# Attention over ragged batches: the transpose of x moves from TensorE to the DMA crossbar, behind a casting load

## Chip, cores, metric

The kernel runs on one core of one Trainium2 chip. The metric is the device time of one execution in microseconds (us). Every comparison is with runs of the kernel before on the same chip. The engines are called by the names of the profile: PE (TensorE), PEld (its weight loads), DVE (VectorE), ACT (ScalarE), POOL (GpSimd), SP (the queue that issues DMAs here).

## The reference

There are 32 batches of 512 rows and 512 columns, with 8 heads of 64. Rows past a batch's length count neither as keys nor in the output. Input and output are float32.

```python
for b in range(batch):
    x_b = x[b, :lengths[b]]
    q, k, v = np.split(np.matmul(x_b, w_qkv), 3, axis=-1)      # then split into heads
    scores = scale * np.matmul(q, k.transpose(0, 2, 1))
    attn = softmax(scores)
    output[b, :lengths[b]] = np.matmul(attn, v)                # heads side by side
```

## The kernel before

The program is a software pipeline over batches: step i projects batch i, attends over batch i-1 and normalizes and stores batch i-2. The Tile framework orders the instructions of each engine by itself, so the order on an engine is not the order of the text.

```python
    # ... pools: ps_a 4 PSUM buffers (psa), ps_s 2 (pssc); bx, bqk, bav, bo, epool in SBUF ...
    def dma_x(j, first=False):
        if j < B:
            xnat[j] = bx.tile([P, NT, D], FP32, tag="x_nat", bufs=4, name="x_nat")
            nc.sync.dma_start(out=xnat[j], in_=x[j].rearrange("(t p) d -> p t d", p=P))

    def stage_qkv(b):
        dma_x(b + 3)
        x_nat = xnat[b]
        x16 = bx.tile([P, NT, D], F16, tag="x16")
        nc.vector.tensor_copy(out=x16, in_=x_nat)                     # DVE cast
        xT = bx.tile([P, NC, MAXS], F16, tag="xT")
        for c in range(NC):
            pxt = ps_a.tile([P, NT, P], F16, tag="psa")
            for t in range(NT):
                nc.tensor.transpose(pxt[:, t, :], x16[:, t, c * P : (c + 1) * P], ident_f16)
            nc.scalar.copy(out=xT[:, c, :], in_=pxt.rearrange("p t q -> p (t q)"))
        for m in range(2 * NC):
            pq = ps_a.tile([P, MAXS], FP32, tag="psa")                # 4 matmuls over c
            # ...
            nc.vector.tensor_copy(out=qkT[:, m, :], in_=pq)
        # ... v: 4 tiles pv of 4 matmuls each, masked by DVE into v_aug ...

    def stage_attn(b):
        def emit_scores(i):                # a pair of heads
            ep = epool.tile([P, 2, NT, MAXS], F16, tag="et")
            for kt in range(NT):
                psc = ps_s.tile([P, 2, MAXS], FP32, tag="pssc")
                # ... two matmuls psc, one for each head ...
                nc.scalar.activation(out=ep[:, :, kt, :], in_=psc, func=AF.Exp, scale=scale)
        # ... emit_av(i): 8 matmuls pav, DVE copies them into avout ...

    def stage_out(b):
        # ... 32 PE transposes pot, DVE: den, rcp, out_nat (product) ...
        nc.sync.dma_start(out=out[b].rearrange("(t p) d -> p t d", p=P), in_=out_nat)
```

The names in what follows: pxt are the transposes of x and xT their copies; pq and pv are the projections; psc are the scores, ep their exps; pav is the weighted sum over v and avout its copy; pot are the transposes of the output and out_nat the normalized output. A transition is the stretch from the last pav of one attention to the pq of the next batch.

The softmax here doesn't subtract the row's maximum and nothing guards it: scores larger than these inputs give would overflow.

Of the kernel before, what the change touches and what calls it, by code (L numbers as in the profile page):

```python
# [9 lines left out]
FP32 = mybir.dt.float32  # L10
F16 = mybir.dt.float16
# [4 lines left out]
P = 128  # L16
# [5 lines left out]
def kernel(  # L22
# [8 lines left out]
    nc = tc.nc  # L31
    B, MAXS, D = x.shape
    NT = MAXS // P
    NC = D // P
# [5 lines left out]
    bx = ctx.enter_context(tc.tile_pool(name="bx", bufs=2))  # L40
# [5 lines left out]
    ps_a = ctx.enter_context(tc.tile_pool(name="ps_a", bufs=4, space=bass.MemoryType.PSUM))  # L46
    ps_s = ctx.enter_context(tc.tile_pool(name="ps_s", bufs=2, space=bass.MemoryType.PSUM))

    xnat = [None] * B

    def dma_x(j, first=False):
        if j < B:
            xnat[j] = bx.tile([P, NT, D], FP32, tag="x_nat", bufs=4, name="x_nat")
            nc.sync.dma_start(
                out=xnat[j], in_=x[j].rearrange("(t p) d -> p t d", p=P)
            )

    dma_x(0)
    len64 = const.tile([1, B], mybir.dt.int64)
    nc.sync.dma_start(out=len64, in_=lengths.unsqueeze(0))  # L60
    dma_x(1)
    dma_x(2)

    ident = const.tile([P, P], FP32)
    make_identity(nc, ident)
    ident_f16 = const.tile([P, P], F16)
# [4 lines left out]
    for c in range(NC):  # L71
# [18 lines left out]
        out=kmask,  # L90
# [6 lines left out]
        out=qbig,  # L97
# [8 lines left out]
    avout_t = [None] * B  # L106

    def stage_qkv(b):
        dma_x(b + 3)
        x_nat = xnat[b]  # L110
        x16 = bx.tile([P, NT, D], F16, tag="x16")
        nc.vector.tensor_copy(out=x16, in_=x_nat)  # L112

        xT = bx.tile([P, NC, MAXS], F16, tag="xT")
        for c in range(NC):
            pxt = ps_a.tile([P, NT, P], F16, tag="psa")
            for t in range(NT):
                nc.tensor.transpose(  # L118
                    pxt[:, t, :], x16[:, t, c * P : (c + 1) * P], ident_f16
                )  # L120
            nc.scalar.copy(out=xT[:, c, :], in_=pxt.rearrange("p t q -> p (t q)"))  # L121

        qkT = bqk.tile([P, 2 * NC, MAXS], F16, tag="qkT")
        qkT_t[b] = qkT
        for m in range(2 * NC):
            pq = ps_a.tile([P, MAXS], FP32, tag="psa")
            for c in range(NC):
                nc.tensor.matmul(  # L128
                    pq,
                    w_r[:, c, m * P : (m + 1) * P],  # L130
                    xT[:, c, :],
                    start=(c == 0),
                    stop=(c == NC - 1),
                )
            nc.vector.tensor_copy(out=qkT[:, m, :], in_=pq)  # L135

        v_aug = bav.tile([P, NT, NH, HD + 1], F16, tag="vaug")
        vaug_t[b] = v_aug
        for t in range(NT):
            pv = ps_a.tile([P, D], FP32, tag="psa")  # L140
            for c in range(NC):
                nc.tensor.matmul(  # L142
                    pv,
                    xT[:, c, t * P : (t + 1) * P],
                    w_r[:, c, 2 * D : 3 * D],
                    start=(c == 0),
                    stop=(c == NC - 1),
                )
            nc.vector.tensor_scalar_mul(  # L149
                v_aug[:, t, :, 0:HD],  # L150
                pv.rearrange("p (h d) -> p h d", d=HD),
                kmask[:, t, b : b + 1],
            )
        nc.vector.tensor_copy(  # L154
            out=v_aug[:, :, :, HD],
            in_=kmask[:, :, b].unsqueeze(2).broadcast_to([P, NT, NH]),
        )
# [52 lines left out]
    def stage_out(b):  # L210
        avout = avout_t[b]
        avout_t[b] = None
        out_nat = bo.tile([P, NT, D], FP32, tag="out_nat")
        for qt in range(NT):
            den8 = sml.tile([P, NH], FP32, tag="den8")
            rcp8 = sml.tile([P, NH], FP32, tag="rcp8")
            pot = ps_a.tile([P, NH, HD + 2], F16, tag="psa")
            for h in range(NH):
                nc.tensor.transpose(  # L219
                    pot[:, h, 0 : HD + 1],  # L220
                    avout[0 : HD + 1, h, qt * P : (qt + 1) * P],
                    ident_f16[0 : HD + 1, 0 : HD + 1],
                )
            nc.vector.tensor_scalar(
                out=den8,
                in0=pot[:, :, HD],
                scalar1=qbig[:, qt, b : b + 1],
                scalar2=None,
                op0=ALU.add,
            )  # L230
            nc.vector.reciprocal(out=rcp8, in_=den8)
            nc.vector.tensor_tensor(  # L232
                out=out_nat[:, qt, :].rearrange("p (h d) -> p h d", d=HD),
                in0=pot[:, :, 0:HD],
                in1=rcp8.unsqueeze(2).broadcast_to([P, NH, HD]),
                op=ALU.mult,
            )
        nc.sync.dma_start(out=out[b].rearrange("(t p) d -> p t d", p=P), in_=out_nat)

    for i in range(B + 2):  # L240
        if i < B:
            stage_qkv(i)
        if 1 <= i <= B:
            stage_attn(i - 1)
        if i >= 2:
            stage_out(i - 2)
# [3 lines left out]
_INS = ['x', 'w_qkv', 'lengths', 'n_heads']  # L250
_OUTS = [((32, 512, 512), 'float32')]
#: Inputs that are plain numbers.
_NUMBERS = {'n_heads': 8}


# [26 lines left out]
```

## Time and profile before

The first three runs gave a median of 948.09 us (946.94 to 950.38). The profiled one has a span of 945.1 us.

| what | before | read from |
|---|---|---|
| PE, ACT, DVE busy | 94%, 58%, 63% | page, busy time |
| two periods of the pipeline (two batches) | 56.43 us | timeline: starts of pv |
| pq and pv of a batch on PE | 6.6 us, 3.45 us | chain of waits |
| one exp in an unbroken row | 0.925 us (12.02 us for 13) | timeline of ACT |
| first pv starts at | 32.18 us | timeline |

The page, cut: the engines' busy time; the one DMA queue of the loads and stores (packets, MB, share of the DMA engines' time); the chain that ended last, by engine and by line.

```profile
PE 891.2 (94%) x5120; PEld 363.4 (38%) x5120; DVE 592.6 (63%) x1094; ACT 547.5 (58%) x645; POOL 1.1 (0%) x8
...
q1 hardware_dynamic: 34370, 70.26, 21.2%
...
PE 83%; ACT 10%; DVE 3%; issue 2%; DMA 1%; POOLq 0%; ACTq 0%; POOL 0%
PE pav L190 25%; PE pq L128 23%; PE psc L173 18%; PE pv L142 12%; ACT ep L180 8%; PE pxt L118 3%; DVE avout L197 2%; PE pot L219 2%; ACT xT L121 2%; DMA w_f<-in_w_qkv_dram 1%; DVE out_nat L232 0%; ACT w_r L74 0%; POOLq L277 0%; ACTq L180 0%; DVE iota_f L86 0%
```

PE is busy nearly throughout, so what it is busy with is what counts; but the profile models the ends of matmuls, and a busy PE that moves at the pace of another engine looks the same. So read the time order as well. The batches come in two kinds of transition, because the order on PE alternates. PE, timeline before, first kind (start, duration, engine, line, operation, output and inputs, shape, count; in brackets idle time and who ended it):

```profile
402.13 0.61 PE L173 MATMUL psc<-qkT 64*128 64x512 f16 x4
402.90 0.40 PE L118 MATMUL pxt<-ident_f_95,x_3802 128*128 128x128 f16 x4 [0.17 <-DVE out_nat L232]
...
403.83 0.39 PE L173 MATMUL psc<-qkT 64*128 64x512 f16 x2
404.17 0.87 PE L118 MATMUL pxt<-ident_f_95,x_3802 128*128 128x128 f16 x8
...
405.59 0.37 PE L173 MATMUL psc<-qkT 64*128 64x512 f16 x1
405.90 6.65 PE L128 MATMUL pq<-xT,w_r 128*128 128x512 f16 x30
```

And the second kind, from the first pxt on:

```profile
431.97 0.40 PE L118 MATMUL pxt<-ident_f_95,x_4081 128*128 128x128 f16 x4
...
432.62 0.40 PE L118 MATMUL pxt<-ident_f_95,x_4081 128*128 128x128 f16 x4
...
433.27 0.80 PE L118 MATMUL pxt<-ident_f_95,x_4081 128*128 128x128 f16 x8
433.91 1.03 PE L128 MATMUL pq<-xT,w_r 128*128 128x512 f16 x4
```

In both, the 16 transposes pxt are mixed with the first score matmuls psc of the next attention, and the projection pq comes behind. ACT over the same stretch:

```profile
402.62 1.02 ACT L180 ACTIVATE ep<-psc 128x1024 f16<-128x1024 f32 x1 [2.68 <-PE psc L173]
403.54 1.07 ACT L121 COPY xT<-pxt 128x512 f16<-128x512 f16 x2
404.49 1.05 ACT L180 ACTIVATE ep<-psc 128x1024 f16<-128x1024 f32 x1
405.40 1.11 ACT L121 COPY xT<-pxt 128x512 f16<-128x512 f16 x2
...
416.36 12.02 ACT L180 ACTIVATE ep<-psc 128x1024 f16<-128x1024 f32 x13 [8.92 <-PE psc L173]
...
445.27 11.11 ACT L180 ACTIVATE ep<-psc 128x1024 f16<-128x1024 f32 x12 [8.81 <-PE psc L173]
```

ACT's four xT copies stand among the exps of the transition.

### The profile page before, as it was taken

How to read it: one execution, taken by the hardware profiler on the slowest of the kernel's cores; microseconds unless marked ns; L12 is line 12 of the kernel's file. 1: busy time of each engine (PE TensorE's matmuls, PEld its weight loads, DVE VectorE, ACT ScalarE, POOL GpSimd, SP SyncE). 2: the span in 40 equal slices, each digit the busy share in tenths (PEclk: the TensorE clock that was granted, in tenths of full speed). 3: DMA queues.
4: the chain of work that ended last, by engine and by line, in shares of the span. 5: the costliest groups of instructions: out<-in, count | busy, mean ns of one | idle time of the engine just before them, and what ended most of it. 6: DMA issues, size and time to landing. Idle time of an engine off the chain costs nothing.

```text
span 945.1 us, 12346 instructions
## 1 busy us (share of the span) xinstructions
PE 891.2 (94%) x5120; PEld 363.4 (38%) x5120; DVE 592.6 (63%) x1094; ACT 547.5 (58%) x645; POOL 1.1 (0%) x8
## 2 busy tenths in 40 slices
PE   2999999999999999999999999999999999999995
PEld 1433434433334433334433334433334433344332
DVE  2745667756667665567756667665566656666555
ACT  3177555576565567455576565567554575645764
POOL 0000000000000000000000000000000000000000
PEclk9899999999999999999999999999999999999997
DMA  9410222220222220222220222220122110111102
GB/s 330 159 45 1 89 89 89 90 72 31 76 90 89 89 89 23 68 90 89 90 72 32 76 89 90 89 82 25 72 90 89 45 45 1 45 45 45 45 26 108
DMA packets 34426, 71.05 MB, mean 75 GB/s; under 512 B 1090, under 2 KB 1090, under 8 KB 34370
## 3 DMA queue, kind: packets, MB, share of 16 engines
q1 hardware_dynamic: 34370, 70.26, 21.2%
q8 instruction: 40, 0.66, 0.3%
q14 instruction: 16, 0.13, 0.0%
HBM read 36.70 MB, written 33.55 MB: 74 GB/s over the span
## 4 chain that ended last, share of the span: by engine, by line
PE 83%; ACT 10%; DVE 3%; issue 2%; DMA 1%; POOLq 0%; ACTq 0%; POOL 0%
PE pav L190 25%; PE pq L128 23%; PE psc L173 18%; PE pv L142 12%; ACT ep L180 8%; PE pxt L118 3%; DVE avout L197 2%; PE pot L219 2%; ACT xT L121 2%; DMA w_f<-in_w_qkv_dram 1%; DVE out_nat L232 0%; ACT w_r L74 0%; POOLq L277 0%; ACTq L180 0%; DVE iota_f L86 0%
## 5 line engine op out<-in xcount | busy, mean ns | idle before, releaser
L180 ACT ACTIVATE ep<-psc 128x1024 f16<-128x1024 f32 x512 | 484.1, 1072 | 355.1 <-PE psc L173 355.1
L197 DVE CAST avout<-pav 65x512 f16<-65x512 f32 x256 | 172.9, 686 | 243.5 <-PE pav L190 243.5
L190 PE MATMUL pav<-ep,v_aug 128*65 128x512 f16 x1024 | 297.0, 388 | 0.0
L128 PE MATMUL pq<-xT,w_r 128*128 128x512 f16 x1024 | 239.5, 388 | 7.3 <-ACT w_r L74 7.2
L173 PE MATMUL psc<-qkT 64*128 64x512 f16 x1024 | 215.5, 385 | 17.0 <-ACT ep L180 13.1
L135 DVE CAST qkT<-pq 128x512 f16<-128x512 f32 x256 | 171.2, 689 | 58.9 <-PE pq L128 57.2
L128 PEld LDWEIGHTS <-w_r 128*128 128x128 f16 x1024 | 98.3, 100 | 128.6 <-issue 16.6
L190 PEld LDWEIGHTS <-v_aug 128*65 128x65 f16 x1024 | 84.2, 110 | 125.7 <-issue 100.1
L173 PEld LDWEIGHTS <-qkT 64*128 64x128 f16 x1024 | 60.5, 93 | 180.3 <-issue 170.9
L142 PE MATMUL pv<-w_r,xT 128*128 128x512 f16 x512 | 115.7, 379 | 0.0
L149 DVE TENSOR_SCALAR v_aug<-pv,kmask 128x512 f16<-128x512 f32 x128 | 96.4, 753 | 16.0 <-PE pv L142 5.5
L121 ACT COPY xT<-pxt 128x512 f16<-128x512 f16 x128 | 70.6, 603 | 22.6 <-PE pxt L118 22.0
L142 PEld LDWEIGHTS <-xT 128*128 128x128 f16 x512 | 50.1, 98 | 60.4
L219 PE MATMUL pot<-ident_f_95,avout 65*128 65x65 f16 x1024 | 45.9, 194 | 2.8 <-DVE out_nat L232 1.4
L219 PEld LDWEIGHTS <-avout 65*128 65x128 f16 x1024 | 38.9, 98 | 19.6 <-issue 7.8
L118 PE MATMUL pxt<-ident_f_95,x_129 128*128 128x128 f16 x16 | 1.9, 308 | 11.7 <-DVE ident_f_95 L67 11.7
L74 ACT CAST w_r<-w_f 128x1536 f16<-128x1536 f32 x4 | 5.8, 1488 | 5.3 <-DMA w_f<-in_w_qkv_dram 5.3
L154 DVE CAST v_aug<-kmask 128x32 f16<-128x32 f32 x32 | 7.4, 230 | 0.0
L118 PEld LDWEIGHTS <-x_129 128*128 128x128 f16 x16 | 1.7, 142 | 11.6 <-DVE x_129 L112 7.4
L112 DVE CAST x_129<-x_nat 128x2048 f16<-128x2048 f32 x1 | 1.2, 1227 | 6.1 <-DMA x_nat<-in_x_dram 6.1
L89 DVE TENSOR_TENSOR kmask<-iota_f,len_f 128x128 f32<-128x128 f32 x1 | 0.3, 292 | 5.1 <-POOL len_f L81 5.1
L86 DVE CAST iota_f<-iota_i 128x4 f32<-128x4 int32 x1 | 0.2, 246 | 3.8 <-POOL iota_i L84 3.8
(490 smaller groups left out, 262.4 us busy)
## 6 DMA issues: line engine op xcount, KB each, us to landing
x_nat<-in_x_dram SPq DMA_DIRECT2D x32, 1024.0 KB, 6.5
out_dram<-out_nat SPq DMA_DIRECT2D x32, 1024.0 KB, 4.9
w_f<-in_w_qkv_dram SPq DMA_DIRECT2D x4, 768.0 KB, 8.9
len_84<-in_lengths_dram SPq DMA_DIRECT2D x1, 0.2 KB
```

What stands on the lines that cost most here:

```text
L118: nc.tensor.transpose(pxt[:, t, :], x16[:, t, c * P : (c + 1) * P], ident_f16)
L121: nc.scalar.copy(out=xT[:, c, :], in_=pxt.rearrange("p t q -> p (t q)"))
L128: nc.tensor.matmul(pq, w_r[:, c, m * P : (m + 1) * P], xT[:, c, :], start=(c == 0), stop=(c == NC - 1),)
L135: nc.vector.tensor_copy(out=qkT[:, m, :], in_=pq)
L142: nc.tensor.matmul(pv, xT[:, c, t * P : (t + 1) * P], w_r[:, c, 2 * D : 3 * D], start=(c == 0), stop=(c == NC - 1),)
L149: nc.vector.tensor_scalar_mul(v_aug[:, t, :, 0:HD], pv.rearrange("p (h d) -> p h d", d=HD), kmask[:, t, b : b + 1],)
L154: nc.vector.tensor_copy(out=v_aug[:, :, :, HD], in_=kmask[:, :, b].unsqueeze(2).broadcast_to([P, NT, NH]),)
L173: nc.tensor.matmul(psc[:, par, :], qkT[rq : rq + 64, NC + i, kt * P : (kt + 1) * P], qkT[rq : rq + 64, i, :], start=True, stop=True,)
L180: nc.scalar.activation(out=ep[:, :, kt, :], in_=psc, func=AF.Exp, scale=scale)
L190: nc.tensor.matmul(pav[0 : HD + 1, :], v_aug[:, kt, h, :], ep[:, par, kt, :], start=(kt == 0), stop=(kt == NT - 1),)
L197: nc.vector.tensor_copy(out=avout[0 : HD + 1, h, :], in_=pav[0 : HD + 1, :])
L219: nc.tensor.transpose(pot[:, h, 0 : HD + 1], avout[0 : HD + 1, h, qt * P : (qt + 1) * P], ident_f16[0 : HD + 1, 0 : HD + 1],)
```

## The change

Its intent is to take 16 transposes a batch off PE, four PSUM copies off ACT and one cast off DVE, and to let the DMA engines do all three. The load is issued on POOL's queue and casts to fp16; four crossbar transposes on SP's queue then build xT. The Trainium skill, "DMA: Bandwidth & Descriptors", section "SWDGE vs HWDGE vs iDMA", ties the cast to POOL's queue and the plain transpose to SP's or ACT's, which is why two queues are needed. Stores move to POOL's queue as well, so that they don't stand between transposes.

```diff
     def dma_x(j, first=False):
         if j < B:
-            xnat[j] = bx.tile([P, NT, D], FP32, tag="x_nat", bufs=4, name="x_nat")
-            nc.sync.dma_start(
-                out=xnat[j], in_=x[j].rearrange("(t p) d -> p t d", p=P)
-            )
+            x16 = bx.tile([P, NT, D], F16, tag="x16", bufs=3, name="x16")
+            nc.gpsimd.dma_start(
+                out=x16, in_=x[j].rearrange("(t p) d -> p t d", p=P)
+            )
+            xT = bx.tile([P, NC, MAXS], F16, tag="xT", bufs=3, name="xT")
+            for t in range(NT):
+                nc.sync.dma_start_transpose(
+                    out=xT[:, :, t * P : (t + 1) * P], in_=x16[:, t, :]
+                )
+            xnat[j] = xT
 # ... dma_x(2) at the start goes away ...
     def stage_qkv(b):
-        dma_x(b + 3)
-        x_nat = xnat[b]
-        # ... cast, 16 transposes, 4 copies, as above ...
+        dma_x(b + 2)
+        xT = xnat[b]
 # ...
-        nc.sync.dma_start(out=out[b].rearrange("(t p) d -> p t d", p=P), in_=out_nat)
+        nc.gpsimd.dma_start(out=out[b].rearrange("(t p) d -> p t d", p=P), in_=out_nat)
```

More of the change, by code (lines that the diff above doesn't have):

```diff
@@ L61 @@
     dma_x(1)
-    dma_x(2)
     ident = const.tile([P, P], FP32)
@@ L108, in stage_qkv @@
     def stage_qkv(b):
-        dma_x(b + 3)
-        x_nat = xnat[b]
-        x16 = bx.tile([P, NT, D], F16, tag="x16")
-        nc.vector.tensor_copy(out=x16, in_=x_nat)
-        xT = bx.tile([P, NC, MAXS], F16, tag="xT")
-        for c in range(NC):
-            pxt = ps_a.tile([P, NT, P], F16, tag="psa")
-            for t in range(NT):
-                nc.tensor.transpose(
-                    pxt[:, t, :], x16[:, t, c * P : (c + 1) * P], ident_f16
-                )
-            nc.scalar.copy(out=xT[:, c, :], in_=pxt.rearrange("p t q -> p (t q)"))
+        dma_x(b + 2)
+        xT = xnat[b]
         qkT = bqk.tile([P, 2 * NC, MAXS], F16, tag="qkT")
```

## The prediction

> **What bounds the kernel now.** The page gives PE 94% busy, ACT 58%, DVE 63%, DMA about a fifth; granted clock 0.98. The timeline shows a period of 56.4 us for two batches (28.2 us each). One batch on PE: query/key projection (pq) 6.6 us and value projection (pv) 3.45 us, both back to back on PE; attention, 12.5 to 13 us, in which a pair of psc and two pav take 0.92 us, which is also ACT's pace for one exp (12.0 us for 13), so PE and ACT are about even there; and a transition of about 5 us: 32 pot transposes, 16 pxt transposes, the next batch's first psc pairs. In the transition the chain of waits goes PE psc, ACT ep, ACT xT, ACT ep, PE pq: the xT copies stand between the exps that free psc's two buffers. Over the span the chain has pxt with 3% and xT with 2%.
>
> **What the change removes.** Per batch: 16 pxt on PE (four take 0.33 to 0.38 us on the chain, so about 1.4 us), 4 xT copies on ACT (pairs of 0.97 to 1.1 us, so about 2.1 us), one DVE cast of 1.23 us (DVE has idle time: worth nothing). PE's order in the built program shows the rest unchanged: pot, three psc, pq, pv.
>
> Critical share: even batches go from psc at 402.2 through two exps and two copies to pq at 405.9; without the copies and pxt only one exp (1.02 us) is left before the third psc, so about 1.8 us is saved. Odd batches: pq starts at 434.07, and would start at about 432.4: 1.6 us. Estimate 1.7 us x 32 = 54 us.
>
> **What it adds.** Per batch one casting load on GpSimd's queue (1 MB read, 0.5 MB written) and four crossbar transposes of 128x512 fp16 on SP's. No trace here has a crossbar transpose. The Trainium skill, "VectorE: DVE Perf Modes", section "The three transpose paths", gives 1309 ns for 128x128 by DMA crossbar and 390 ns on TensorE. Estimate from it: at worst 16 x 1.31 = 21 us a batch if nothing overlaps, under the 26.5 us period left. With three xT buffers, the transposes of batch j start when pq/pv of batch j-3 is done, about two periods ahead. So I expect them hidden and PE never waiting for xT in the steady state. The output leaves through GpSimd behind loads that were ready earlier; no stall expected.
>
> Start: PE's first full pq group waits for the last w_r cast (25.4 us). In the new order on SP the last two w_f loads stand behind eight transposes, which wait for two GpSimd loads. Before, they were issued at 15.8 us; I expect 16 to 22. Cost 0 to 8 us, say 3. End: the last output through GpSimd, about 1 us more.
>
> **Prediction.** 948 - 54 + 3 + 1 = 898 us, 80% range 884 to 917. Faster by over 2%: 0.87; within 2%: 0.06; slower: 0.07.
>
> **What would show it right.** Timeline: period near 26.5 us; pxt and xT gone; ACT's exps in the transition back to back; PE's waits name no DMA apart from the start. DMA view: four transposes of a batch landing within about 20 us. Start: last w_r cast between 25 and 33 us.
>
> **What would make it wrong.** Transposes of over 6.6 us each, in series: then PE waits for xT in every batch and the kernel is DMA-bound, perhaps slower than before. SP's issue of the transposes taking microseconds each, delaying the weights. Slow casting loads. Or the transition being held by the DVE chain (den, rcp, out_nat, 3.4 us), which frees the PSUM buffers that pq takes: then the gain is nearer 1 us a batch.

## More of the kernel before

A period is the time from the first pv of a batch to the first pv of the next; it is called undisturbed where no stretch of half clock falls into it.

After pv, exps run in one unbroken row: 13 of them in 12.02 us after the first kind of transition, 12 in 11.11 us after the second.

## The result, and the profile after

The changed kernel took 904.66 us (median of 4 runs, 900.37 to 906.16), the kernel before in the same rounds 948.51 us. The ratio is 0.9529, with a 95% interval of 0.9499 to 0.9558. The profiled span fell from 945.1 to 903.6 us.

The page after, the same parts (POOL's queue is q0, SP's is q1):

```profile
PE 852.7 (94%) x4608; PEld 332.8 (37%) x4608; DVE 551.1 (61%) x1062; ACT 484.4 (54%) x517; POOL 49.5 (5%) x72
...
q0 software_dynamic: 25600, 50.34, 22.5%
q1 hardware_dynamic: 70210, 19.94, 11.2%
...
PE 53%; issue 21%; ACT 18%; DVE 3%; DMA 2%; SPq 1%; POOL 1%; POOLq 0%; ACTq 0%
```

PE is as busy as before, in share. The DMA engines went from 21.2% to 33.7% (both queues), and PE waits for them only at the start. That is read from PE's own waits (who waited for whom: us in total, times, longest us):

```profile
PE pq L122 <- DMA xT<-x_82: 16.4, 1, 16.4
PE psc L167 <- ACT ep L174: 9.3, 17, 0.9
PE pq L122 <- ACT w_r L79: 7.1, 2, 6.9
```

The only wait for a DMA, 16.4 us, is the start; so is the third line, where the casts of w_r wait for the last loads of the weights. How fast the crossbar works is seen in two timelines. SP's queue, the four transposes of a batch, and POOL's queue, the load that waits until they have freed x16:

```profile
399.55 5.12 SPq L59 DMA_TRANSPOSE xT<-x_3757  x4
```

```profile
406.45 0.74 POOL L54 DMA_DIRECT2D x_4528<-in_x_dram  x1 [15.87 <-DMA xT<-x_3757]
```

SP issues four transposes in 5.12 us, and the load that waits for their completion is released at 406.45, 6.9 us after the first was issued. A period is 27 us, so the crossbar needs a quarter of it.

PE after, the end of the two kinds of transition:

```profile
415.02 0.60 PE L167 MATMUL psc<-qkT 64*128 64x512 f16 x3
415.71 1.89 PE L122 MATMUL pq<-xT,w_r 128*128 128x512 f16 x8
...
441.44 0.39 PE L167 MATMUL psc<-qkT 64*128 64x512 f16 x2
442.32 0.37 PE L167 MATMUL psc<-qkT 64*128 64x512 f16 x1 [0.50 <-ACT ep L174]
442.63 7.08 PE L122 MATMUL pq<-xT,w_r 128*128 128x512 f16 x32
```

ACT after:

```profile
427.01 12.02 ACT L174 ACTIVATE ep<-psc 128x1024 f16<-128x1024 f32 x13 [9.63 <-PE psc L167]
441.25 1.94 ACT L174 ACTIVATE ep<-psc 128x1024 f16<-128x1024 f32 x2 [2.21 <-PE psc L167]
453.52 12.94 ACT L174 ACTIVATE ep<-psc 128x1024 f16<-128x1024 f32 x14 [10.33 <-PE psc L167]
```

pxt and the copies are gone, and pq follows psc at once (in the first kind one last psc, at 417.53, stands between the pq groups). But compare the unbroken rows of exps. After the first kind of transition there are 13 again (12.02 us), after the second kind there are now 14 (12.94 us) where there were 12. What this does is seen in the chain of waits over that one period, with the row of 12 before (441.2 to 468.8) and the row of 14 after (449.5 to 476.7):

```profile
by line: PE pav L190 25.2%; PE pq L128 24.6%; PE psc L173 16.5%; PE pv L142 12.5%; ACT ep L180 10.8%; DVE avout L197 4.9%; ACT xT L121 3.5%; PE pot L219 1.5%; issue 1.1%; ACTq L180 0.1%
by line: ACT ep L174 45.2%; PE pq L122 27.2%; PE pv L136 12.7%; DVE avout L191 4.7%; issue 3.0%; DVE out_nat L226 2.5%; PE psc L167 2.4%; PE pav L184 1.4%; DVE den_4214 L218 0.5%; DVE den_4228 L218 0.5%; DVE rcp_4215 L225 0.4%
```

Before, attention on the chain is PE's psc and pav; after, in this period, it is ACT's exps. In the period with the row of 13 the chain goes over psc and pav after the change too (ACT ep 7.8%).

The starts of pv, read from the timeline, give the account of the profiled runs:

| stretch | before | after | difference | predicted |
|---|---|---|---|---|
| to the first pv | 32.18 | 34.92 | +2.7 | +3 |
| first to last pv (31 periods) | 866.44 | 820.69 | -45.8 | -54 (32 x 1.7) |
| last pv to the end | 46.48 | 47.99 | +1.5 | +1 |

The undisturbed periods alternate. Before they are 28.86 and 27.57 us, after 26.51 and 27.14 us; the mean falls from 28.22 to 26.83, by 1.39 us. Some periods are longer by 1.3 to 1.7 us. They are told under the first experiment.

### The profile page after: what moved, and what is told of

Its sections match the earlier page's. It is cut to its first block, busy times and chain, and to the rows that moved or that the text cites. A ratio compares the mean times of both kernels' runs of the same rounds, so it can differ in the third digit from the quotient of the medians.

```text
span 903.6 us, 11385 instructions
## 1 busy us (share of the span) xinstructions
PE 852.7 (94%) x4608; PEld 332.8 (37%) x4608; DVE 551.1 (61%) x1062; ACT 484.4 (54%) x517; POOL 49.5 (5%) x72
## 4 chain that ended last, share of the span: by engine, by line
PE 53%; issue 21%; ACT 18%; DVE 3%; DMA 2%; SPq 1%; POOL 1%; POOLq 0%; ACTq 0%
PE pq L122 21%; ACT ep L174 18%; PE pav L184 13%; PE pv L136 10%; PE psc L167 9%; DVE avout L191 2%; PE pot L213 1%; SPq L59 1%; DVE out_nat L226 1%; DMA x_82<-in_x_dram 1%; DMA w_f<-in_w_qkv_dram 1%; POOL out_dram L232 1%; ACT w_r L79 0%; POOLq L271 0%; DVE qkT L129 0%
## 5 line engine op out<-in xcount | busy, mean ns | idle before, releaser
L174 ACT ACTIVATE ep<-psc 128x1024 f16<-128x1024 f32 x512 | 477.2, 1082 | 382.8 <-PE psc L167 382.8
L191 DVE CAST avout<-pav 65x512 f16<-65x512 f32 x256 | 169.7, 684 | 271.6 <-PE pav L184 271.5
L184 PE MATMUL pav<-ep,v_aug 128*65 128x512 f16 x1024 | 305.0, 389 | 1.5
L122 PE MATMUL pq<-xT,w_r 128*128 128x512 f16 x1024 | 238.8, 390 | 24.8 <-DMA xT<-x_82 16.4
L184 PEld LDWEIGHTS <-v_aug 128*65 128x65 f16 x1024 | 80.5, 110 | 124.4 <-issue 109.7
L213 PE MATMUL pot<-ident_f_103,avout 65*128 65x65 f16 x1024 | 50.7, 194 | 2.3 <-DVE out_nat L226 1.6
L213 PEld LDWEIGHTS <-avout 65*128 65x128 f16 x1024 | 41.6, 98 | 27.6 <-issue 14.6
L232 POOL DMA_DIRECT2D out_dram<-out_nat x32 | 24.3, 761 | 431.7 <-DVE out_nat L226 410.0
L54 POOL DMA_DIRECT2D x_1444<-in_x_dram x1 | 0.7, 740 | 25.4 <-DMA xT<-x_673 25.4
L54 POOL DMA_DIRECT2D x_7098<-in_x_dram x1 | 0.7, 740 | 17.2 <-DMA xT<-x_6327 17.2
L54 POOL DMA_DIRECT2D x_4528<-in_x_dram x1 | 0.7, 740 | 15.9 <-DMA xT<-x_3757 15.9
```

What stands on the lines that cost most here:

```text
L122: nc.tensor.matmul(pq, w_r[:, c, m * P : (m + 1) * P], xT[:, c, :], start=(c == 0), stop=(c == NC - 1),)
L184: nc.tensor.matmul(pav[0 : HD + 1, :], v_aug[:, kt, h, :], ep[:, par, kt, :], start=(kt == 0), stop=(kt == NT - 1),)
L191: nc.vector.tensor_copy(out=avout[0 : HD + 1, h, :], in_=pav[0 : HD + 1, :])
L213: nc.tensor.transpose(pot[:, h, 0 : HD + 1], avout[0 : HD + 1, h, qt * P : (qt + 1) * P], ident_f16[0 : HD + 1, 0 : HD + 1],)
L232: nc.gpsimd.dma_start(out=out[b].rearrange("(t p) d -> p t d", p=P), in_=out_nat)
```

## The experiments

Three questions: which of the things removed was worth the 1.39 us; which half of the change did it; and what holds the period now. The theory at the start (A) was that of the prediction: copies and transposes shared the critical path in the transition. The rivals: PE alone (B), since 16 pxt, at 0.33 to 0.38 us for four on the chain, are about 1.4 us by themselves; and the queues and the DVE cast (C).

All runs, ratios to the kernel before. "Period" is the mean of the undisturbed periods; "half clock" counts the stretches of half clock on PE between 40 us and the last attention, in the profiled execution alone.

| run | median us | ratio, 95% interval | period us | half clock | first pv us |
|---|---|---|---|---|---|
| before | 947.4 to 948.7 | 1 | 28.22 | 5 | 32.2 |
| the change | 904.7 | 0.953 (0.950 to 0.956) | 26.83 | 3 | 34.9 |
| e1_pe_back | 946.0 | 0.999 (0.997 to 1.000) | 27.83 | 9 | 34.2 |
| e2_act_back | 904.9 | 0.955 (0.953 to 0.958) | 26.82 | 1 | 36.7 |
| e3_cast_only | 942.7 | 0.995 (0.992 to 0.998) | 28.22 | 6 | 26.0 |
| e4_xbar_only | 909.2 | 0.960 (0.958 to 0.962) | 27.05, see there | 3 | 33.1 |
| e5_w_on_act | 897.2 | 0.946 (0.942 to 0.949) | 26.82 | 1 | 30.0 |
| e6_half_exp (wrong result) | 853.0 | 0.898 (0.894 to 0.902) | 25.32 | 0 | 37.7 |
| e7_spread | 878.3 | 0.926 (0.922 to 0.929) | 26.10 | 0 | 34.9 |
| e8_spread_w | 873.6 | 0.921 (0.917 to 0.924) | 26.10 | 0 | 30.7 |
| e9_before_spread | 927.4 | 0.977 (0.974 to 0.981) | 27.81 | 0 | 33.2 |
| e10_both_free | 957.2 | 1.008 (1.003 to 1.013) | 28.06 | 11 | 35.0 |

### e1_pe_back: PE's transposes put back, nobody reads them

```diff
         xT = xnat[b]
+        for c in range(NC):
+            pxt = ps_a.tile([P, NT, P], F16, tag="psa")
+            for t in range(NT):
+                nc.tensor.transpose(pxt[:, t, :], x16s[b][:, t, c * P : (c + 1) * P], ident_f16)
```

> The changed kernel with the 16 TensorE transposes of each batch put back; what they write is read by nobody, so ACT's copies stay away. Result correct. Theory A (the gain comes from the transition between two batches, where PE's transposes and ACT's copies shared the critical path): part of the 44 us comes back, 10 to 30 us, so 914 to 934 us. Rival B (PE alone: 16 transposes at 0.087 us are 1.4 us, which is all that a batch became shorter): all comes back, 940 to 950 us. Rival C (the gain comes from the loads and stores leaving SP's queue and from the DVE cast): nothing comes back, 900 to 909 us.

Measured: 945.98 us, as rival B has it. But the period tells more than the time: it is 27.83 us, so the undisturbed period went up by 1.0 us, not by 1.39. That is a mean over two orders on PE. All periods of this run have the order of the second kind (13 exps in the row, PE waits 0.50 us for an exp in the transition); beside the changed kernel's period of that kind, 26.51 us, the 16 pxt cost 1.32 us, all of it between the last pav and the next pv, so nearly their whole time on PE. The rest of the 41 us comes from nine stretches in which PE had half its clock, against three in the changed kernel's profile. One of them, by windows of one us (from:to, length, busy time of each engine, granted clock, DMA share, GB/s):

```profile
405.00:406.00 1.00, 1.00 (x9) 0.66 (x8) 1.00 (x3) 0.69 (x2) 0.00 (x0) 0.57 0.09 16
406.00:407.00 1.00, 1.00 (x10) 0.83 (x8) 0.21 (x1) 0.56 (x1) 0.00 (x0) 0.50 0.00 0
407.00:408.00 1.00, 1.00 (x4) 0.33 (x3) 0.00 (x0) 0.00 (x0) 0.81 (x2) 0.50 0.00 0
408.00:409.00 1.00, 1.00 (x5) 0.45 (x4) 0.37 (x1) 0.00 (x0) 0.68 (x1) 0.72 0.62 20
409.00:410.00 1.00, 1.00 (x7) 0.41 (x6) 0.93 (x3) 0.00 (x0) 0.00 (x0) 1.00 0.51 29
```

At half clock the granted share is 0.50, so 0.57, 0.50, 0.50 and 0.72 make 0.86 + 1 + 1 + 0.56 = 3.4 us. The period in which it falls is 29.45 us, 1.6 us longer than its neighbours. Nine of these instead of three account for about 10 us, and 31 times 1.0 us for the rest. The Trainium skill, "TensorE: Matmul & The Clock Gate", section "Part 1: The HAM clock gate (the "warmup" mystery)", describes a free-running window of 3413 ns, after which a PE seen as idle gets half clock; the 3.4 us here agree with it. All eight of them in the profiles before and after fall in the batches with the transition with single psc between pot (the second kind), in which PE also waits 0.50 us for an exp. What in it counts as idle is not shown.

### e2_act_back: ACT's copies put back, without PE's transposes

```diff
-        xT = xnat[b]
+        xT = bx.tile([P, NC, MAXS], F16, tag="xT2", bufs=2)
+        for c in range(NC):
+            nc.scalar.copy(out=xT[:, c, :], in_=xnat[b][:, c, :])
```

> The changed kernel with four ACT copies a batch put back (xT copied once more by ACT into a second tile that the matmuls read; source in SBUF instead of PSUM), no TensorE transposes. Result correct. Theory A: the copies stand between the exps again, 15 to 45 us come back, 919 to 949 us. Rival B (PE alone): 900 to 909 us. Rival C (queues and DVE cast): 900 to 909 us.

Measured: 904.93 us and a period of 26.82 us, nothing came back in the mean. Theory A falls in this form. Three of the four copies do stand between two exps of the transition, as ACT's timeline shows, and cost nothing there:

```profile
402.30 12.92 ACT L176 ACTIVATE ep<-psc 128x1024 f16<-128x1024 f32 x14
414.96 1.78 ACT L117 COPY xT<-xT 128x512 f16<-128x512 f16 x3
416.50 2.07 ACT L176 ACTIVATE ep<-psc 128x1024 f16<-128x1024 f32 x2
```

A caveat: these copies wait for no transpose and were free to move (the fourth went ahead of attention's row of exps), while those of before were tied between pxt and pq. And the mean hides two things that cancel. The fourth copy puts off the row: its first exp starts 0.60 us after the end of pv instead of 0.36. In the kind of period whose other parts are as in the changed kernel, that is the whole difference (26.74 against 26.51 us); the other kind has another order of psc and pot on PE and is shorter for it (26.89 against 27.14 us).

### e10_both_free: both put back, untied

The edits of the two runs above together.

> The changed kernel with both put back but not tied together: the 16 TensorE transposes of each batch, read by nobody, and the four ACT copies (of xT, which the matmuls then read). Result correct. The kernel of before has an undisturbed period of 28.2 us, the one with the TensorE transposes alone 27.8 us, the one with the copies alone 26.8 us. Theory F (the last 0.4 us come from the tie: the copy waits for the transpose and pq for the copy): 27.8 us, as with the transposes alone, 940 to 950 us. Rival G (ACT's load counts once PE has the transposes too): 28.1 to 28.3 us, 950 to 962 us.

Measured: 957.22 us, slower than before, with 11 stretches of half clock; the period is 28.06 us. The time fits rival G; the period falls just short of its range, 0.23 us over the transposes alone and 0.16 us under the kernel before. The trace shows where the 0.23 us are: the row's first exp starts 0.60 us after the end of pv instead of 0.36, since the fourth copy stands before it, as in e2_act_back, and the other parts of the period agree with e1_pe_back within 0.05 us. So it is the place of one copy on ACT; the three in the transition cost nothing here either. The 0.16 us that are left to the kernel before, where copies were tied and the order on PE alternates, stay open.

### e3_cast_only and e4_xbar_only: the halves

```diff
 # e3: the casting load and the store on POOL's queue; instead of the crossbar:
+                nc.tensor.transpose(pxt[:, t, :], x16[:, t, c * P : (c + 1) * P], ident_f16)
+            nc.scalar.copy(out=xT[:, c, :], in_=pxt.rearrange("p t q -> p (t q)"))
 # e4: load and store on SP as before; two batches ahead:
+            nc.vector.tensor_copy(out=x16, in_=xnat[j])
+            for t in range(NT):
+                nc.sync.dma_start_transpose(out=xT[:, :, t * P : (t + 1) * P], in_=x16[:, t, :])
```

> Half of the change: casting loads and stores on GpSimd's queue, but TensorE transposes and ACT copies as before; the DVE cast stays away. Result correct. Theories A and B: the time of before, 940 to 953 us, because the DVE cast was off the critical path. Rival C: most of the gain, under 920 us.

Measured: 942.66 us. The period is that of before, 28.22 us; the gain of 0.5% lies in the start, where the first pv comes at 26.0 us instead of 32.2, since the loads of x no longer stand before the weights on one queue (the first weights land at 5.4 us instead of 13.7). In its place the DVE cast was worth nothing, and rival C falls.

> The other half: plain fp32 loads and the stores on SP's queue and the DVE cast as before, but crossbar transposes. Result correct. Theories A and B: the time of the changed kernel, 897 to 912 us (the start may differ by some us, since SP issues everything). Rival C: near the time of before, over 930 us.

Measured: 909.17 us. The crossbar alone brings nearly all of the gain. It is 4 to 6 us short of the changed kernel (by medians or by ratios), and the periods say where: 26.51 us and 27.58 or 27.70 us alternate, where the changed kernel has 26.51 and 27.14, until the last batch has been cast; then it is 26.51 and 27.14 here too. The cast in this kernel waits for x16 to come free, and then lands in the middle of attention, ahead of the copies of avout. DVE's timeline in a period of 27.70 us, and PE's over the same stretch:

```profile
567.66 0.69 DVE L202 CAST avout<-pav 65x512 f16<-65x512 f32 x1 [2.32 <-PE pav L195]
571.09 1.23 DVE L62 CAST x<-x_nat 128x2048 f16<-128x2048 f32 x1 [2.74 <-DMA xT<-x]
572.23 1.88 DVE L202 CAST avout<-pav 65x512 f16<-65x512 f32 x3
...
572.96 0.38 PE L195 MATMUL pav<-ep,v_aug 128*65 128x512 f16 x1 [0.58 <-DVE avout L202]
```

DVE waits 2.74 us for the transposes to release x16 and casts for 1.23 us; the copies of three pav come only then, and PE waits 0.58 us for the first of them, which is the difference between 27.70 and 27.14 us. In the other kind of period, 26.51 us, the cast stands in attention too, but PE doesn't wait there. So a cast that costs nothing in one place of DVE's order costs about half a microsecond in another.

### e5_w_on_act: the weights on another queue

The start of the changed kernel, timeline:

```profile
9.86 5.19 SPq L59 DMA_TRANSPOSE xT<-x_82  x4
...
16.41 3.16 PE L122 MATMUL pq<-xT,w_r 128*128 128x512 f16 x8 [16.41 <-DMA xT<-x_82]
...
20.41 0.98 SPq L78 DMA_DIRECT2D w_f<-in_w_qkv_dram  x2
...
27.07 1.47 ACT L79 CAST w_r<-w_f 128x1536 f16<-128x1536 f32 x1 [0.67 <-DMA w_f<-in_w_qkv_dram]
```

The last two weight loads (SPq, 20.41) stand behind eight transposes, and their second cast ends at 28.5 us; PE waits for it.

```diff
-        nc.sync.dma_start(out=w_f, in_=w_qkv[c * P : (c + 1) * P, :])
+        nc.scalar.dma_start(out=w_f, in_=w_qkv[c * P : (c + 1) * P, :])
```

> The changed kernel, but the four weight loads are issued on ACT's queue instead of SP's, where the last two stand behind eight transposes. Result correct. If those eight transposes cost the start (first pv at 34.9 us in the changed kernel, 26.0 us in the run with casting loads and TensorE transposes, where only the crossbar is missing), the first pv comes at 25 to 28 us and the time falls by 6 to 10 us, 895 to 899 us. Rival: the start is held by the transposes themselves or by the first load, and nothing changes: 902 to 906 us.

Measured: 897.18 us, as expected in time. The first pv comes at 30.0 us, later than expected: pq now waits for xT until 20.88 us, and then runs through. The last two weight loads, issued at 13.15 and 13.69 us, are now in flight beside the first batch's transposes, of which the last lands at 20.75 us instead of 16.28. Its profiled span is 8.2 us shorter than that of the changed kernel: 4.9 us are the start, and 3.3 us are two stretches of half clock that it doesn't have, so only the first belongs to the edit for sure. Transposes stay on one queue here. The Trainium skill, "DMA: Bandwidth & Descriptors", section "Silent corruption: two transposing streams in flight at once", warns against spreading them over two; no run here shows it.

### e6_half_exp: half of ACT's work taken away

```diff
-                    out=ep[:, :, kt, :], in_=psc, func=AF.Exp, scale=scale
+                    out=ep[:, 0, kt, :], in_=psc[:, 0, :], func=AF.Exp, scale=scale
 # and pav reads ep[:, 0, kt, :] for both heads
```

> WRONG RESULT ON PURPOSE: the changed kernel with exp taken of one head of each two (512 columns instead of 1024), the other head's pav reads the same tile. PE's work is unchanged, ACT's exps are about halved. Theory D (in the changed kernel the pace of attention, 0.92 us for a pair of psc and two pav, is ACT's; PE alone needs 0.87): the period falls from 26.8 to 25 to 26 us and the time to 850 to 880 us. Rival E (PE sets the pace all along; ACT's exps wait for it): 899 to 909 us.

Measured: 852.95 us, period 25.32 us in every batch; the result is wrong. With PE's work the same, 1.5 us a batch were ACT's. Theory D holds: in the changed kernel attention runs at ACT's pace for a part.

### e7_spread, e8_spread_w: exps moved to where ACT stood idle

```diff
             nc.vector.tensor_copy(out=qkT[:, m, :], in_=pq)
+            if b >= 1:
+                emit_scores_kt(b - 1, m // NT, m % NT)      # psc pair and exp of the batch before
 # stage_attn then emits only the scores of head pairs 2 and 3
```

> The changed kernel with half of the psc pairs and exps of a batch (8 of 16) emitted among the eight pq groups of the next batch, where ACT stood idle for 9 to 10 us. Same work, result correct. Theory D: attention is no longer at ACT's pace, period 25.2 to 26.2 us, 855 to 885 us. Rival E (PE sets the pace): 899 to 912 us, since PE's work is the same.

Measured: 878.30 us, correct, period 26.10 us in every batch, without one stretch of half clock between start and end. ACT's timeline shows the unbroken row cut to 8 exps, and the others between groups of pq:

```profile
442.54 7.44 ACT L174 ACTIVATE et<-pssc 128x1024 f16<-128x1024 f32 x8 [2.92 <-PE pssc L167]
...
458.23 1.02 ACT L174 ACTIVATE et<-pssc 128x1024 f16<-128x1024 f32 x1 [1.89 <-PE pssc L167]
459.53 1.02 ACT L174 ACTIVATE et<-pssc 128x1024 f16<-128x1024 f32 x1 [0.27 <-PE pssc L167]
```

Half of the 1.5 us that the run before allowed is gained. The rest is not explained here.

> The two before it together (exps spread, weights on ACT's queue). Result correct. If both are right their savings add: the time of the spread kernel less 6 to 10 us. If only one is right, the time of that one.

Measured: 873.60 us, correct, 0.921 of the time before and the fastest correct kernel. The weights' queue is worth 4.7 us beside the spread, a little less than expected, and the start moved by 4.2 us: the savings add, once half clock is out of the account.

### e9_before_spread: what is the crossbar worth then?

The spread edit on the kernel before.

> The kernel of before (TensorE transposes, loads and stores on SP) with its exps spread over pq as in the spread kernel. Result correct. What is the crossbar worth when attention is no longer at ACT's pace (changed kernel with spread: 26.10 us, 878.3 us)? If PE's work is what counts then: 16 times 0.087 us, period 27.4 to 27.7 us, 915 to 930 us. If the copies on ACT count as well (they would now stand beside exps under pq): 28 us or more, over 935 us.

Measured: 927.42 us, period 27.81 us. The time is that of the first case (PE's work is what counts); the period lies 0.11 us above its range and 0.19 us below the second. Against the spread kernel with the crossbar it is 1.71 us a period, where the unspread pair differs by 1.39. So when attention no longer absorbs part of it, the crossbar change is worth its 16 pxt and 0.3 us more. The stretches of half clock are absent here too, although PE does all its transposes: transposes alone don't bring them.

## Why the prediction was right, and where it was off

1. **The time.** 904.66 us lies in the range; the centre was 7 us low. Direction and size of the gain were right, the size in part by luck: the two halves of the estimate were off by -1.4 and +0.75 us a batch (point 4), and these errors cancel in part.
2. **The DMA side was right.** Four transposes took 5.12 us to issue and were done 6.9 us after the first issue, against the estimate of 21 us at worst, from the skill's figure, and PE waited for a DMA only at the start.
3. **Start and end were right:** +2.7 and +1.5 us against +3 and +1. The reason given for the start, weights behind transposes, is shown by the e5_w_on_act run.
4. **The term that was mis-sized is "1.7 us x 32 = 54 us".** It measured 1.39 us in the undisturbed period. By kind of transition: the prediction had 1.8 us for the batches with the first kind and 1.6 us for those with the second. Measured: 0.43 us (27.57 to 27.14) and 2.35 us (28.86 to 26.51). Take the unbroken row of exps out of each: 27.57 - 11.11 = 16.46 us became 27.14 - 12.94 = 14.20 us, and 28.86 - 12.02 = 16.84 us became 26.51 - 12.02 = 14.49 us. So everything outside the row became shorter by 2.3 us in both, more than forecast; but in every second batch the row took in two exps more, 1.83 us, and there it came to lie on the chain of waits. Before, those two had run in the second kind of transition, with psc between the pxt; without pxt the order on PE goes to pq at once, and the two psc pairs come after pv; so part of the second kind's 2.35 us is work that only moved. Marked on PE, the stretch from the last pav to the next pv fell from 11.74 to 9.97 us in the first kind, by 1.77 us as forecast for it; but attention before it, from pv to the last pav, grew from 15.83 to 17.18 us. The prediction took the transition as the only place that changes and attention as fixed: that is the step that failed. The runs with half exps and with spread exps show that ACT's pace in attention costs time, 1.5 us a batch of which 0.7 were got back. The danger named last in the prediction is seen too: in the first kind after the change the chain goes from the last pav over DVE's avout, den, rcp and out_nat (466.9 to 469.4) to pq. What that costs was not tested.
5. **The copies alone were the wrong culprit.** "The xT copies stand between the exps that free psc's two buffers" is true of the trace, but put back alone, untied, they cost nothing in the mean (26.82 us), and the three that stand between exps cost nothing where the order on PE is otherwise the same. PE's transposes alone cost 1.0 of the 1.39 us in the mean, 1.32 us between periods of the same kind. What the tie between pxt, copy and pq costs was not tested by itself. Nor was it tested what the waits of pxt for DVE's out_nat cost before (0.17 and 0.20 us in the first kind, 5.5 us in the whole execution), which went away with pxt.
6. **"DVE has idle time: worth nothing"** was right for the cast where it stood (28.22 us with and without it), but not as a rule: in the e4_xbar_only run it came to lie in attention, and the period is 0.2 us longer in the mean.
7. **Not foreseen at all:** the stretches of half clock. Between before and after they make about 2 us (5 x 1.35 against 3 x 1.69), but they make e1_pe_back look like a full return to the time before.

## What to carry to other kernels

Work taken off a bottleneck engine shortens the stretch in which it stood, but the other work that ran in its shadow must go somewhere: count, before and after, how much of the next engine's work is left for the stretch that this engine paces. Compare undisturbed periods and not only total times, since a clock stretch can fill exactly the gap that you look for. And when an engine stands idle for 9 us of a 27 us period while it paces another part, moving its work there (here exps under the projection) may be worth more than half of the change that you came for (26 us here, beside 44; about 5 of the 26 are three stretches of half clock that the spread kernel doesn't have).

## What the Trainium skill lacked or had wrong

- "VectorE: DVE Perf Modes", "The three transpose paths", gives 1309 ns for a 128x128 transpose by the crossbar. Here one 128x512 transpose, four times as much, is issued every 1.26 us and lands 2.5 us after its issue (median of most batches), so 0.32 us per 128x128 in a row of them. Taken as a cost per tile in a row, the page's figure was four times too high here.
- "TensorE: Matmul & The Clock Gate", "Part 1": the length of a half-clock stretch agrees (3.4 us). How many of them come is what I could not foresee from it: 0 to 11 in one execution between kernels whose PE is all 94 or 95% busy, and 11 of them make about 18 us. "Part 4: PE-mode transpose" of the same page says that transposes don't count as PE-busy in the same way. Here a kernel with 48 transposes a batch had none of these stretches (e9_before_spread) and one with the same number had 11 (e10_both_free), so this is not enough to tell when they come.
